# Layer one's key pieces split and stored by batch 0, and a new order of both mixers

## The chip, the cores and the metric

One core of one Trainium2 chip runs the kernel. The metric is the device time of one execution in microseconds; of the kernel before three runs are shown. The core's engines are TensorE (PE in the rows; its weight loads are PEld), VectorE (DVE), ScalarE (ACT), GpSimd (POOL) and SyncE (SP), which here issues all large DMAs, in order.

## What is computed

Two layers of a streaming encoder, on 1024 prompt frames and 8 streams of 16 frames, so 9 tiles of 128 tokens, of width 1024. Everything is float32.

```python
def trunk_layer(x, pos, cache_k, cache_v, pool_prev, conv_prev, ...):
    xn = rms_norm(x, norm_mix)
    q, k, v, u = mixer_inputs(xn, pos, w_in, q_gain, k_gain)   # 512 | 128 | 128 | 512 columns
    attn = window_attention_prompt(q, k, v, sinks)             # or sink_attention over the cache
    pool, new_pool = pool_mixer(u, pool_prev, w_pool, pool_scale)
    x = x + jnp.concatenate([attn, pool], axis=-1) @ w_out
    f, new_conv = conv_ffn(rms_norm(x, norm_ffn), conv_prev, w_up, conv_w, conv_b, w_down)
    x = x + f
```

`pool_mixer` takes running means over 2, 4, 8 and 16 frames; `conv_ffn` multiplies by w_up (1024 x 5632), convolves over 3 frames, gates and multiplies by w_down (2816 x 1024).

## The kernel before, in words

Every large product is made as three: each operand is split into a rounded high part and the remainder (`hi`, `lo`), and `mm3` (products at L154 to L156) issues hi x hi, hi x lo and lo x hi into one accumulator. A weight piece (128 x 512, or two 128 x 256 side by side) is loaded raw by SyncE (`w_dma`, L167; the load is at L218 or L227), cast to its high part by ScalarE (L184) or VectorE (L182) and subtracted by VectorE (L185): `w_split`. A piece with a key is then stored, both parts, 512 KB, in a scratch in DRAM (L188); the next time a piece of that key is wanted, it is loaded from there in one go (L179) and not split. `w_advance` keeps raw loads five pieces and splits three pieces ahead; there are 6 buffers of split pieces (`W`) and 5 raw ones.

Each layer is a mixer and then a feed-forward part of 21 up and 34 down units. The mixer takes the tiles in three batches of three. For batch b the units are called k{b} (query, key and value columns, 12 pieces: 8 of 512 columns and 4 pairs of 256), u{b} (pooling columns, 8 pieces), p{b} (pooling), L (steps of attention for all batches), o{b} (out projection, 16 pieces); n1 to n3 are the input norms of the batches with their transposes (norm multiply L258 on VectorE; the transposes at L278 are evacuated at L281 by ScalarE and L282 by VectorE), m0 to m2 the norms before the feed-forward part. s0 and s1 prepare the operands of its first products: sums and splits of 128 x 1152 (L314 on ScalarE, L315 and L323 on VectorE), and v and w are those products (their evacuations: L938). `par` loads the small parameters: gains (L1261, L1262), sinks (L1263, and L1265 eight times), the pool's scale (L1267), with small multiplies at L1268 to L1270. `sc` loads state rows (L1304), `cw` the convolution's weights (L1285, L1286).

The first three key pieces of batch 0 are used for tile 0, then tile 1, then tile 2, as their norms come (L362 on); from the fourth piece on a unit holds all three tiles.

What sets the order: every unit is a token with a number from `PLAN` (L65 to L68; a pair gives the first number and the step of a stream, `L` the numbers of the tiles, the `e_` entries choose VectorE, 1, or ScalarE, 0, for some copies; `e_w` says how many of every four weight pieces have their high part cast by VectorE, L1444). `arrange` (L45) takes the token with the least number whose forerunners (`pre`) are done. After that the framework's scheduler may shift instructions within each engine's order; each engine runs its own in order. The keys are given by `keyed` in the mixer's function. In layer one (l == 0) batch 0's key pieces get none, so batch 0 splits them and stores nothing, batch 1 loads and splits them again and stores them, and batch 2 loads the stored ones. In layer two, and for the u and o pieces of both layers, the first batch stores.

Of the kernel before, what the change touches and what calls it, by code (L numbers as in the profile page):

```python
# [44 lines left out]
def arrange(tokens, limits):  # L45
# [26 lines left out]
def encoder_kernel(ctx: ExitStack, tc: tile.TileContext, consts, x_prompt, x_sample, cache_k, cache_v,  # L72
# [1280 lines left out]
    for l in range(DEPTH):  # L1353
# [11 lines left out]

        def keyed(x, units, b, l=l):
            if l == 0 and x == "k" and b == 0:
                return units
            for i, w in enumerate(w for u in units for w in u.ws):
                w.key = l, x, i  # L1370
            return units
# [39 lines left out]
        n = [0] * 9  # L1411
# [104 lines left out]
```

## Time and profile before

| | us |
|---|---|
| three runs, median (lowest to highest) | 2229.7 (2226.32 to 2231.16) |
| the profiled execution, its own time | 2223.63 |
| its span in the profile | 2221.8 |
| TensorE busy in the span | 2157.7 (97%) |
| VectorE busy | 1705.8 (77%) |
| ScalarE busy | 966.2 (43%) |
| GpSimd busy | 326.8 (15%) |
| TensorE's clock, mean over the span | 0.995 of full |

Layer one's mixer takes about the first 400 us, layer two's lies between about 1000 and 1500; the rest is the feed-forward parts. Read the busy shares first, then the stretches in which TensorE is not busy, then what it waited for in each of them. A busy TensorE at a granted clock of 0.5 gets half as much done, so the clock's column belongs to the reading.

### The profile page before, as it was taken

What the parts mean: (1) busy time and instruction counts of PE and PEld (TensorE: products, weight loads), DVE (VectorE), ACT (ScalarE), POOL (GpSimd) and SP (SyncE); (2) the same over time, 40 slices, a digit from 0 to 9 for tenths busy, and PEclk for the clock granted to TensorE, in tenths of its full rate; (3) what the DMA queues carried; (4) which work ended last, traced back from release to release, by engine and by line L of the source; (5) the groups of instructions that cost most, each with busy time, mean ns of one, the idle gap of its engine ahead of it and who ended that gap; (6) DMA issues with size and microseconds to landing.
All of it is one profiled execution on the core that took longest, in us unless ns stands there. A gap on an engine that the chain in (4) does not pass through costs nothing.

```text
span 2221.8 us, 36068 instructions
## 1 busy us (share of the span) xinstructions
PE 2157.7 (97%) x13178; PEld 1935.6 (87%) x13178; DVE 1705.8 (77%) x3210; ACT 966.2 (43%) x1797; POOL 326.8 (15%) x499
## 2 busy tenths in 40 slices
PE   7999999999999999999999999989999999999999
PEld 6777867999999998878888887779999999988887
DVE  5775468998999998766556754699898999987663
ACT  4554356443434344443345544564343434353431
POOL 0100001112122323000000000012212232320000
PEclk9999999999999999999999999999999999999999
DMA  7667753222233437958675676532222343488563
GB/s 253 231 215 261 267 183 135 77 87 95 80 118 124 143 126 257 286 173 270 209 253 182 231 244 211 210 112 88 98 77 96 108 150 119 152 280 270 184 192 110
DMA packets 320036, 386.49 MB, mean 174 GB/s; under 512 B 21938, under 2 KB 224386, under 8 KB 319858
## 3 DMA queue, kind: packets, MB, share of 16 engines
q1 hardware_dynamic: 319858, 384.18, 52.3%
q8 instruction: 104, 1.70, 0.3%
q14 instruction: 74, 0.61, 0.1%
HBM read 274.73 MB, written 109.37 MB: 173 GB/s over the span
## 4 chain that ended last, share of the span: by engine, by line
PE 84%; DMA 6%; DVE 4%; ACT 2%; issue 2%; SPq 0%; POOL 0%; DVEq 0%; ACTq 0%; POOLq 0%
PE mm L154 15%; PE mm L156 15%; PE mm L155 15%; PE s L154 11%; PE s L156 11%; PE s L155 11%; PE s L653 2%; DMA B<-gd 1%; DMA raw<-in_w_down_dram 1%; PE tr L640 1%; DMA W<-wd0o 1%; PE tr L278 1%; PE mm L457 1%; PE s L601 1%; PE s L602 1%
## 5 line engine op out<-in xcount | busy, mean ns | idle before, releaser
L154 PE MATMUL mm<-B,W 128*128 128x288 f32 (+1 forms) x1376 | 419.7, 305 | 12.6 <-ACT B L314 10.7
L155 PE MATMUL mm<-B,W 128*128 128x288 f32 (+1 forms) x1376 | 417.8, 304 | 3.7 <-DVE B L315 3.7
L156 PE MATMUL mm<-B,W 128*128 128x288 f32 (+1 forms) x1376 | 417.1, 303 | 0.0
L154 PE MATMUL s<-B,B 128*128 128x512 f32 x704 | 279.1, 397 | 3.8 <-DVE u L1172 1.8
L156 PE MATMUL s<-B,B 128*128 128x512 f32 x704 | 278.6, 396 | 3.9 <-DVE B L1145 3.9
L155 PE MATMUL s<-B,B 128*128 128x512 f32 x704 | 277.9, 395 | 0.0
L154 PEld LDWEIGHTS mm<-B,W 128*128 128x128 f32 x1376 | 260.8, 190 | 17.0 <-ACT B L314 12.6
L155 PEld LDWEIGHTS mm<-B,W 128*128 128x128 f32 x1376 | 260.7, 189 | 5.9 <-DVE B L315 4.6
L156 PEld LDWEIGHTS mm<-B,W 128*128 128x128 f32 x1376 | 260.7, 190 | 0.7 <-issue 0.2
L986 DVE SCALAR_TENSOR_TENSOR B<-B,cvp,B 128x1168 f32<-128x1168 f32 x176 | 250.4, 1427 | 3.1 <-ACT B L984 2.8
L154 PE MATMUL mm<-W,B 128*128 128x512 f32 (+1 forms) x576 | 216.4, 383 | 11.8 <-ACT W L184 3.8
L156 PE MATMUL mm<-W,B 128*128 128x512 f32 (+1 forms) x576 | 215.2, 375 | 0.0
L155 PE MATMUL mm<-W,B 128*128 128x512 f32 (+1 forms) x576 | 214.2, 372 | 0.0
L879 ACT CAST W<-Q 128x512 fp32r<-128x512 f32 x132 | 82.1, 622 | 250.1 <-PE mm L156 166.0
L1144 ACT CAST B<-B 128x256 fp32r<-128x256 f32 (+1 forms) x128 | 97.2, 780 | 208.1 <-DMA B<-gd 70.0
L154 PE MATMUL s<-B,W 128*128 128x288 f32 x576 | 171.0, 297 | 0.0
L155 PE MATMUL s<-B,W 128*128 128x288 f32 x576 | 170.0, 295 | 0.0
L156 PE MATMUL s<-B,W 128*128 128x288 f32 x576 | 170.0, 295 | 0.0
L156 PEld LDWEIGHTS s<-B,B 128*128 128x128 f32 x704 | 132.5, 188 | 36.8 <-DVE B L1145 5.6
L154 PEld LDWEIGHTS s<-B,B 128*128 128x128 f32 x704 | 132.6, 188 | 36.5 <-ACT B L1144 5.2
L155 PEld LDWEIGHTS s<-B,B 128*128 128x128 f32 x704 | 132.6, 188 | 30.8
L880 DVE TENSOR_TENSOR W<-Q,W 128x512 fp32r<-128x512 f32 x132 | 135.8, 1030 | 17.3 <-ACT W L879 17.2
(234 smaller groups left out, 4856.9 us busy)
## 6 DMA issues: line engine op xcount, KB each, us to landing
raw<-in_w_up_dram SPq DMA_DIRECT2D x176, 256.0 KB
raw<-in_w_down_dram SPq DMA_DIRECT2D x154, 256.0 KB
gd<-B SPq DMA_DIRECT2D x44, 576.0 KB
B<-gd SPq DMA_DIRECT2D x32, 576.0 KB
W<-wd0o SPq DMA_DIRECT2D x32, 512.0 KB
W<-wd1o SPq DMA_DIRECT2D x32, 512.0 KB
raw<-in_w_in_dram SPq DMA_DIRECT2D x52, 256.0 KB
W<-wd1k SPq DMA_DIRECT2D x24, 512.0 KB
```

The costliest lines, as they stand in the source:

```text
L154: pe.matmul(out=out, lhsT=a[0], rhs=b[0], start=first, stop=False)
L155: pe.matmul(out=out, lhsT=a[0], rhs=b[1], start=False, stop=False)
L156: pe.matmul(out=out, lhsT=a[1], rhs=b[0], start=False, stop=last)
L278: pe.transpose(out=tr[:, (k - a) * 128:(k - a + 1) * 128], in_=xn[:, k * 128:(k + 1) * 128], identity=ident)
L457: pe.matmul(out=o, lhsT=w.raw, rhs=d, start=True, stop=True)
L601: pe.matmul(out=p[:, i, kr], lhsT=q[:, h], rhs=K[:, g, kr], start=True, stop=False)
L602: pe.matmul(out=p[:, i, kr], lhsT=q[:, h], rhs=K[:, 2 + g, kr], start=False, stop=True)
L653: pe.matmul(out=o, lhsT=V, rhs=H.pop(("p", g, kk)), start=kk == kks[0], stop=kk == 1)
L879: act.copy(out=hi, in_=src)
L880: dve.tensor_tensor(out=lo, in0=src, in1=f32(hi), op=ALU.subtract)
L986: dve.scalar_tensor_tensor(out=c, in0=h[:, j:j + 1168], scalar=cvp[:, j, ct:ct + 1], in1=c, op0=ALU.mult, op1=ALU.add)
L1144: act.copy(out=h, in_=f32(o))
```

## The change

It gives batch 0's key pieces of layer one their key as well: batch 0 splits and stores them, batches 1 and 2 load them. It sets the numbers of nearly all streams of both mixers anew, chooses the engine of some copies differently (in both layers key columns to VectorE, value columns to ScalarE; in layer one u columns to ScalarE, and every fourth cast of a weight piece to VectorE; in layer two `e_x1` to ScalarE and `e_x2` to VectorE), and makes the unit w.5 wait for `cw` and `sc`. Of the table the row of layer one is shown, and not that of layer two.

```diff
-    dict(k0=(12.35, 0.15), u0=(27.6, 1.13), k1=(35.46, 2.26), u1=(78.0, 4.62), o0=(92.76, 2.89), k2=(160.39, 1.54), u2=(167.47, 3.15), o1=(177.0, 4.09), o2=(235.74, 4.2), p0=(40.1, 3.5), p1=(86.68, 12.45), p2=(194.05, 11.9), n1=(-86.25, 2.26), n2=(26.8, 3.63), n3=(92.6, 1.1), m0=(218.99, 3.57), m1=(260.89, 0.13), m2=(181.58, 0.95), d=(-13.48, 3.86), L=(26.9, 49.72, 64.52, 85.45, 108.8, 144.29, 158.38, 183.7, 209.44, 245.41), cw=(259.88, 23.53), sc=(227.68, 60.94), s0=(257.44, 3.18), s1=(268.93, 2.61), v=(209.05, 0.65), w=(316.25, 1.16), upw=(342.36, 0.16), e_q=0, e_k=0, e_v=1, e_u=1, e_k2=1, e_qt=0, e_pt0=0, e_pt1=0, e_ps0=1, e_ps1=1, e_ks=0, e_w=0, e_x0=1, e_x1=0, e_x2=0),
+    dict(k0=(0.4, 2.37), u0=(34.1, 0.93), k1=(35.52, 2.03), u1=(80.99, 4.42), o0=(76.31, 4.58), k2=(160.39, 1.54), u2=(167.28, 3.02), o1=(177.22, 4.01), o2=(234.36, 9.42), p0=(40.1, 2.0), p1=(77.15, 12.45), p2=(193.68, 11.66), n1=(-114.15, 0.88), n2=(25.73, 3.64), n3=(96.31, 1.04), m0=(215.0, 3.57), m1=(265.16, 0.34), m2=(195.73, 0.23), d=(5.52, 6.56), L=(26.9, 49.72, 64.52, 85.8, 108.91, 144.29, 149.46, 186.79, 209.44, 245.41), cw=(351.65, 368.58), sc=(220.46, 49.37), s0=(257.44, 3.51), s1=(242.24, 0.26), v=(182.04, 25.01), w=(370.59, 1.67), upw=(408.93, 0.1), e_q=0, e_k=1, e_v=0, e_u=0, e_k2=1, e_qt=0, e_pt0=0, e_pt1=0, e_ps0=1, e_ps1=1, e_ks=0, e_w=1, e_x0=1, e_x1=0, e_x2=0),
...
@@ -1363,9 +1363,7 @@
                 q = list((pre or {}).get(i, ())) + ([f"{st}.{i - 1}"] if i else [])
                 add(f"{st}.{i}", k + i * step, u, q, (res or {}).get(i))
 
-        def keyed(x, units, b, l=l):
-            if l == 0 and x == "k" and b == 0:
-                return units
+        def keyed(x, units, l=l):
             for i, w in enumerate(w for u in units for w in u.ws):
                 w.key = l, x, i
             return units
@@ -1400,8 +1398,8 @@
             nn = f"n{b + 1}.5"
             kres = {7: {"qkv": 3}, 11: {"V": 3}}
             kpre = {0: [nn, f"k{b - 1}.11"], 11: ["par"]} if b else {0: ["n1.1"], 1: ["n1.3"], 2: ["n1.5"], 11: ["par"]}
-            stream(f"k{b}", keyed("k", kvq_units(l, b), b), kpre, kres)
-            stream(f"u{b}", keyed("u", u_units(l, b), b), {0: [nn] + (["d.9"] if l else []), 3: [f"p{b - 1}.3"] if b else [], 7: [f"p{b}.0"] + (["spl"] if b == 2 else [])}, {7: {"T6": -6}})
+            stream(f"k{b}", keyed("k", kvq_units(l, b)), kpre, kres)
+            stream(f"u{b}", keyed("u", u_units(l, b)), {0: [nn] + (["d.9"] if l else []), 3: [f"p{b - 1}.3"] if b else [], 7: [f"p{b}.0"] + (["spl"] if b == 2 else [])}, {7: {"T6": -6}})
             if b == 2:
                 toks[-5].pre += ("spl",)
             stream(f"p{b}", [pool_unit(l, b, g) for g in range(4)], {0: [f"u{b}.3", "par"], 2: [f"u{b}.7"]}, {0: {"T6": 3}})
@@ -1419,7 +1417,7 @@
             add(f"L.{i}", key, f, ([f"L.{i - 1}"] if i else ["par"] + (["d.9"] if l else [])) + list(pre), res)
             lastidx[t] = i
         for b in range(3):
-            ou = keyed("o", out_units(l, b), b)
+            ou = keyed("o", out_units(l, b))
             pre = {0: [f"p{b}.3"], 4: [f"L.{lastidx[3 * b + 2]}"]}
             stream(f"o{b}", ou, pre, {15: {"T6": -6}})
         for nm, f1, f2, pre in (("cw", conv_load, conv_cols, []), ("sc", sconv_load, sconv_cols, [kc1])):
@@ -1434,7 +1432,7 @@
             add(f"upw{i}", pl["upw"][0] + pl["upw"][1] * i, lambda l=l, i=i: up_advance(l, i), ["o2.10"])
         for s, k in ((0, "v"), (1, "w")):
             for n, x in enumerate((0, 1, 7, 4, 8, 10, 2)):
-                pre = [f"s{s}.{x}", "o2.15"] + ([f"{k}.{n - 1}"] if n else ["v.6"] if s else [])
+                pre = [f"s{s}.{x}", "o2.15"] + ([f"{k}.{n - 1}"] if n else ["v.6"] if s else []) + (["cw", "sc"] if s and n == 5 else [])
                 add(f"{k}.{n}", pl[k][0] + pl[k][1] * n, up_first(l, s, n), pre)
         ev = arrange(toks, {"T6": 18, "qkv": 4, "V": BUFS["V"]})
         for t in ev:
```

In counts, over the whole program: raw loads of key pieces 52 before, 40 now; loads of split layer-one key pieces 12 before, 24 now, stores of them 12 in both; subtractions at L185 84 before, 72 now; casts at L182 (VectorE) 8 before, 19 now, at L184 (ScalarE) 76 before, 53 now; copies of u columns on VectorE 8 before, none now. TensorE's products are the same in number.

SyncE at the beginning, before (`raw` are weight pieces in the order of use, `snk`, `gain` and `V` the parameters, `B` the input):

```order
9 L1349 DMA cst<-in_consts_dram 128x464
10 L1261 DMA gain<-in_q_norm_dram 128x64
11 L1262 DMA gain<-in_k_norm_dram 128x64
12 L1263 DMA snk<-in_attn_sinks_dram 128x8
13 L1265 DMA snk<-in_attn_sinks_dram 16x1 x8
14 L1267 DMA V_268<-in_pool_scale_dram 4x128
15 L218 DMA raw_276<-in_w_in_dram 128x512
16 L247 DMA B_250<-in_x_prompt_dram 128x1024
17 L247 DMA B_252<-in_x_prompt_dram 128x1024
18 L247 DMA B_254<-in_x_prompt_dram 128x1024
19 L218 DMA raw_278<-in_w_in_dram 128x512
```

The same place now:

```order
9 L1349 DMA cst<-in_consts_dram 128x464
10 L218 DMA raw_250<-in_w_in_dram 128x512
11 L218 DMA raw_252<-in_w_in_dram 128x512
12 L1261 DMA gain<-in_q_norm_dram 128x64
13 L1262 DMA gain<-in_k_norm_dram 128x64
14 L1263 DMA snk<-in_attn_sinks_dram 128x8
15 L1265 DMA snk<-in_attn_sinks_dram 16x1 x2
16 L188 DMA wd0k_86<-W_254 128x1024
17 L218 DMA raw_258<-in_w_in_dram 128x512
18 L1265 DMA snk<-in_attn_sinks_dram 16x1
19 L188 DMA wd0k_87<-W_260 128x1024
20 L218 DMA raw_264<-in_w_in_dram 128x512
```

The fourth and fifth raw pieces have moved ahead of the parameters, and from then on a store of a split key piece (`wd0k`) stands ahead of each further raw load.

VectorE ahead of batch 1's norms, before, from the evacuation of the first u columns on (raw_633, raw_689 and raw_691 are batch 1's first key pieces; `sA` and `D` belong to pooling):

```order
60 L149 COPY u_645<-mm_544 128x384
61 L185 TENSOR_TENSOR W_733<-raw_633,W_733 128x512
62 L282 TENSOR_TENSOR B_614<-tr_622,B_611 128x3x128
63 L414 COPY uh<-u_645 128x15
64 L425 TENSOR_TENSOR sA_659<-u_645 128x398
65 L149 COPY u_655<-mm_551 128x384
66 L185 TENSOR_TENSOR W_763<-raw_689,W_763 128x512
67 L429 SCALAR_TENSOR_TENSOR D_662<-sA_659,u_645 128x384
68 L414 COPY uh<-u_655 128x15
69 L185 TENSOR_TENSOR W_858<-raw_691,W_858 128x512
```

The same place now, from the split of the first u piece that stands behind the rotary step of tile 0 (raw_476 and raw_506 are u pieces):

```order
64 L185 TENSOR_TENSOR W_693<-raw_476,W_693 128x512
65 L414 COPY uh<-u_754 128x15
66 L425 TENSOR_TENSOR sA_768<-u_754 128x398
67 L414 COPY uh<-u_764 128x15
68 L429 SCALAR_TENSOR_TENSOR D_771<-sA_768,u_754 128x384
69 L185 TENSOR_TENSOR W_744<-raw_506,W_744 128x512
70 L436 TENSOR_TENSOR D_771<-sA_768,cst 128x15
71 L437 TENSOR_TENSOR D_771<-D_771,u_754 128x15
72 L425 TENSOR_TENSOR sA_846<-u_764 128x398
73 L400 MEMSET u_873 128x15
74 L149 CAST B_590<-tr_591 128x4x128
```

The splits of key pieces and the copies of u columns are gone from between the pooling steps. Before, 26 of the subtractions at L185 stand ahead of the second tile's first evacuation in batch 1 and 30 ahead of the third tile's last; now it is 20 and 20. Of the copies of u columns 4 stood there, of casts at L182 none; now it is none and 6.

VectorE at the end of layer one's mixer, before (the first three rows are the last norms' multiplies, L938 evacuates first products, L315 and L323 are the second half's sums and splits):

```order
620 L258 SCALAR_TENSOR_TENSOR B_3915<-B_3556,st_3916,B_3309 128x1024
621 L258 SCALAR_TENSOR_TENSOR B_3921<-B_3558,st_3922,B_3309 128x1024
622 L258 SCALAR_TENSOR_TENSOR B_3927<-B_3560,st_3928,B_3309 128x1024
623 L938 TENSOR_TENSOR B_4029<-mm_4016,PT_4011 128x288
624 L938 TENSOR_TENSOR PT_4011<-s_4034,PT_4011 128x288
625 L938 TENSOR_TENSOR PT_4065<-mm_4052,PT_4011 128x288
626 L938 TENSOR_TENSOR PT_4011<-mm_4071,PT_4011 128x288
627 L938 TENSOR_TENSOR B_4085<-mm_4071,PT_4065 128x288
628 L938 TENSOR_TENSOR B_4085<-s_4087,PT_4065 128x288
629 L938 TENSOR_TENSOR B_4029<-mm_4101,PT_4011 128x288
630 L315 TENSOR_TENSOR B_4116<-B_3725,B_4115 128x1152
631 L315 TENSOR_TENSOR B_4120<-B_3733,B_4119 128x1152
```

The same place now:

```order
613 L258 SCALAR_TENSOR_TENSOR B_3919<-B_3538,st_3920,B_3234 128x1024
614 L258 SCALAR_TENSOR_TENSOR B_3925<-B_3540,st_3926,B_3234 128x1024
615 L938 TENSOR_TENSOR B_3987<-mm_3974,PT_3911 128x288
616 L938 TENSOR_TENSOR PT_3911<-s_3992,PT_3911 128x288
617 L315 TENSOR_TENSOR B_4007<-B_3653,B_4006 128x1152
618 L938 TENSOR_TENSOR PT_4055<-mm_4042,PT_3911 128x288
619 L315 TENSOR_TENSOR B_4011<-B_3661,B_4010 128x1152
620 L938 TENSOR_TENSOR PT_3911<-mm_4061,PT_3911 128x288
621 L938 TENSOR_TENSOR B_3987<-mm_4091,PT_3911 128x288
622 L315 TENSOR_TENSOR B_4015<-B_3945,B_4014 128x1152
623 L880 TENSOR_TENSOR W_4172<-raw_4149,W_4172 128x512
624 L938 TENSOR_TENSOR B_3987<-mm_4119,PT_3911 128x288
```

The first two splits of the second half stand between the evacuations and no longer behind all of them; two evacuations of the first half (`mm_4061` again, and `s_4077`) have gone behind the sums.

## Rows read from the trace of the kernel before

**Rows 1.** The page's first part: busy us of each engine, share, instructions.
```profile
PE 2157.7 (97%) x13178; PEld 1935.6 (87%) x13178; DVE 1705.8 (77%) x3210; ACT 966.2 (43%) x1797; POOL 326.8 (15%) x499
```

**Rows 2.** Stretches of 25 us; columns: us, busy (instructions) by engine, PEclk, DMA share, GB/s.
```profile
0.00:25.00 25.00, 12.50 (x48) 9.81 (x49) 11.93 (x25) 11.15 (x21) 1.97 (x8) 0.93 0.73 256
...
50.00:75.00 25.00, 22.92 (x135) 20.64 (x133) 23.02 (x72) 14.31 (x35) 2.91 (x2) 1.00 0.77 270
...
375.00:400.00 25.00, 18.23 (x104) 15.98 (x103) 23.86 (x29) 14.34 (x22) 2.69 (x5) 0.86 0.04 11
...
1450.00:1475.00 25.00, 22.27 (x140) 19.32 (x139) 24.21 (x31) 13.62 (x28) 6.03 (x6) 1.00 0.47 157
1475.00:1500.00 25.00, 19.01 (x124) 17.35 (x123) 23.64 (x29) 14.39 (x20) 0.00 (x0) 0.86 0.06 17
```

**Rows 3.** Timeline of SyncE at the beginning: start, us, engine, line, operation, count.
```profile
9.31 4.90 SPq L1265 DMA_DIRECT2D snk<-in_attn_sinks_dram  x8
...
14.66 0.36 SPq L218 DMA_DIRECT2D raw<-in_w_in_dram  x1
```

**Rows 4.** Timelines of ScalarE, VectorE, TensorE, 16 to 19 us; in brackets idle before, releaser.
```profile
17.48 0.62 ACT L184 CAST W<-raw 128x512 fp32r<-128x512 f32 x1 [2.30 <-DMA raw<-in_w_in_dram]
...
16.50 1.28 DVE L258 SCALAR_TENSOR_TENSOR B<-B,st,B 128x1024 f32<-128x1024 f32 x1 [0.67 <-POOL st L257]
...
18.15 0.79 PE L154 MATMUL mm<-W,B 128*128 128x512 f32 x1 [3.00 <-ACT W L184]
18.75 1.48 PE L278 MATMUL tr<-cst,B 128*128 128x128 f32 x6
```

**Rows 5.** Stretches of 2 us at the beginning; columns as in group 2.
```profile
18.00:20.00 2.00, 1.85 (x8) 1.67 (x8) 1.87 (x2) 0.48 (x2) 0.47 (x1) 0.50 1.02 381
```

**Rows 6.** Stretches holding batch 1's first key pieces, layer one, then layer two.
```profile
64.00:88.00 24.00, 19.57 (x95) 14.99 (x94) 21.58 (x77) 13.69 (x41) 4.52 (x3) 0.93 0.27 94
1171.00:1191.00 20.00, 19.01 (x102) 14.68 (x101) 14.88 (x47) 10.98 (x25) 0.55 (x1) 1.00 0.18 59
```

**Rows 7.** Timeline of TensorE in batch 1's stage of layer one.
```profile
75.70 0.60 PE L278 MATMUL tr<-cst,B 128*128 128x128 f32 x2 [2.15 <-DVE B L282]
```

**Rows 8.** Groups of one line: count, lowest/median/highest ns, first and last start.
```profile
L184 ACT CAST W<-raw x76: 602/621/642, 8.0 to 1274.0; 128x512 fp32r<-128x512 f32 x76
...
L185 DVE TENSOR_TENSOR W<-raw,W x84: 658/691/694, 8.7 to 1275.3; 128x512 fp32r<-128x512 f32 x84
...
L182 DVE CAST W<-raw x8: 418/427/428, 1023.0 to 1264.2; 128x512 fp32r<-128x512 f32 x8
...
L149 DVE COPY u<-mm x8: 541/554/558, 53.2 to 166.8; 128x384 f32<-128x384 f32 x8
...
L188 SPq DMA_DIRECT2D wd0k<-W x12: 326/472/1301, 54.8 to 99.3; - x12
```

**Rows 9.** The DMA view, 0 to 66 us: totals, and two kinds of issues.
```profile
DMA packets 9638, 17.71 MB, mean 268 GB/s; under 512 B 1507, under 2 KB 5290, under 8 KB 9633
...
raw<-in_w_in_dram SPq DMA_DIRECT2D x28, 256.0 KB
...
wd0k<-W SPq DMA_DIRECT2D x5, 512.0 KB
```

**Rows 10.** A stretch of layer two's batch 0; columns as in group 2.
```profile
1136.00:1148.00 12.00, 12.00 (x63) 10.47 (x62) 10.06 (x22) 5.79 (x12) 2.18 (x2) 1.00 1.05 395
```

**Rows 11.** Timelines of SyncE, VectorE and TensorE at the ends of both mixers.
```profile
324.73 7.68 SPq L1304 DMA_DIRECT2D B<-in_state_conv_dram  x8
...
329.78 0.17 DVE L1269 TENSOR_SCALAR snk<-snk 128x8 f32<-128x8 f32 x1 [4.96 <-DMA snk<-in_attn_sinks_dram]
...
381.02 0.40 PE L154 MATMUL mm<-B,W 128*128 128x288 f32 x1 [1.73 <-ACT B L314]
...
1446.53 0.15 DVE L256 TENSOR_SCALAR st<-st 128x1 f32<-128x1 f32 x1 [2.02 <-ACT B L255]
...
1487.17 0.61 PE L154 MATMUL mm<-B,W 128*128 128x288 f32 x1 [3.93 <-ACT B L314]
```

More of the change, by code (lines that the diff above doesn't have):

```diff
@@ L67 @@
-    dict(k0=(-43.86, 0.15), u0=(49.49, 0.1), k1=(26.26, 4.1), u1=(76.32, 4.61), o0=(81.16, 2.69), k2=(139.16, 1.11), u2=(150.18, 5.15), o1=(175.45, 5.19), o2=(244.07, 2.25), p0=(49.92, 3.56), p1=(56.81, 4.29), p2=(193.02, 12.48), n1=(-18.93, 0.85), n2=(30.53, 4.46), n3=(92.15, 1.8), m0=(222.0, 1.72), m1=(234.28, 0.33), m2=(278.02, 1.14), d=(-24.93, 3.08), L=(26.9, 49.72, 64.52, 87.91, 106.15, 148.52, 158.51, 180.13, 216.19, 239.71), cw=(264.41, 12.12), sc=(273.99, 6.32), s0=(264.1, 2.08), s1=(276.75, 4.45), v=(278.27, 0.1), w=(272.47, 516.37), upw=(298.18, 0.41), e_q=0, e_k=0, e_v=1, e_u=0, e_k2=0, e_qt=0, e_pt0=0, e_pt1=0, e_ps0=1, e_ps1=1, e_ks=0, e_w=1, e_x0=0, e_x1=1, e_x2=0),
+    dict(k0=(0.4, 2.37), u0=(34.1, 0.93), k1=(35.52, 2.03), u1=(80.99, 4.42), o0=(76.31, 4.58), k2=(160.39, 1.54), u2=(167.28, 3.02), o1=(177.22, 4.01), o2=(234.36, 9.42), p0=(40.1, 2.0), p1=(77.15, 12.45), p2=(193.68, 11.66), n1=(-114.15, 0.88), n2=(25.73, 3.64), n3=(96.31, 1.04), m0=(215.0, 3.57), m1=(265.16, 0.34), m2=(195.73, 0.23), d=(5.52, 6.56), L=(26.9, 49.72, 64.52, 85.8, 108.91, 144.29, 149.46, 186.79, 209.44, 245.41), cw=(351.65, 368.58), sc=(220.46, 49.37), s0=(257.44, 3.51), s1=(242.24, 0.26), v=(182.04, 25.01), w=(370.59, 1.67), upw=(408.93, 0.1), e_q=0, e_k=1, e_v=0, e_u=0, e_k2=1, e_qt=0, e_pt0=0, e_pt1=0, e_ps0=1, e_ps1=1, e_ks=0, e_w=1, e_x0=1, e_x1=0, e_x2=0),
@@ new lines @@
+    dict(k0=(-19.1, 0.17), u0=(41.72, 0.11), k1=(23.93, 4.64), u1=(76.32, 4.66), o0=(81.16, 2.69), k2=(131.41, 2.01), u2=(159.64, 3.19), o1=(176.74, 5.16), o2=(244.45, 2.2), p0=(50.37, 3.79), p1=(41.63, 2.14), p2=(196.59, 14.02), n1=(-19.61, 0.67), n2=(28.93, 4.45), n3=(97.64, 0.29), m0=(224.51, 0.88), m1=(254.53, 0.73), m2=(277.92, 1.14), d=(-24.93, 2.65), L=(26.9, 49.72, 64.52, 88.15, 105.43, 151.29, 160.24, 182.14, 217.23, 240.57), cw=(253.91, 4.74), sc=(274.24, 6.92), s0=(251.59, 2.11), s1=(265.4, 3.05), v=(280.44, 0.1), w=(269.22, 13783.52), upw=(276.35, 0.22), e_q=0, e_k=1, e_v=0, e_u=0, e_k2=0, e_qt=0, e_pt0=0, e_pt1=0, e_ps0=1, e_ps1=1, e_ks=0, e_w=1, e_x0=0, e_x1=0, e_x2=1),
```

## The prediction

> **What bounds the kernel now.** I began with the busy shares: TensorE is busy 2157.7 of a span of 2221.8 us [rows 1], so 64 us are to be had on it at most, by removing its waits. The table of 25-us stretches says where they lie. The long stages of both feed-forward parts read 25.00 of 25; what is missing lies in the first 25 us (12.50 busy, clock 0.93), at 50 to 75 (22.92), and where a mixer ends: 375 to 400 (18.23, clock 0.86) and 1450 to 1500 (22.27, then 19.01 at clock 0.86) [rows 2]. From 50, 375 and 1450 us on VectorE is nearly full, 23.02, 23.86 and 24.21 of 25: there it sets the pace, and a microsecond taken from it ahead of a late operand is worth about one. ScalarE (14 us of 25) is bound nowhere.
>
> Then the timelines. At the beginning SyncE issues eight tiny loads of sinks from 9.31 to 14.21 and only at 14.66 the next weight load [rows 3]. That piece lands at 17.48, where ScalarE had waited 2.30 us for it, and TensorE stands 3.00 us, until 18.15 [rows 4]; from 18 to 20 its clock is then granted at 0.50, which is 1.2 GHz, the lower of the two levels, where it takes double time [rows 5]. In batch 1's query-key-value stage TensorE is busy 19.57 of 24 us at a clock of 0.93, with VectorE at 21.58 of 24; the same stage of layer two, whose weights had been split and stored by batch 0, reads 19.01 of 20 at 1.00, VectorE 14.88 of 20 [rows 6]. The longest gap there, 2.15 us before 75.70, waits for VectorE's evacuation of transposes (L282) [rows 7]. So this stage is held by VectorE, not by weights or by TensorE.
>
> **The change, part by part.** *Splits.* Batch 1's 12 key pieces are no longer split. Off VectorE go 12 subtractions of 691 ns (8.3 us), off both engines 12 casts, and the new numbers shift casts and evacuations: on VectorE 11 more casts of 427 ns (+4.7) and 8 fewer u evacuations of 554 ns (-4.4), on ScalarE 23 fewer casts of 621 ns (-14.3) [rows 8]. VectorE's sum is -8.0 us. ScalarE's part I cost at nothing: it is covered by TensorE, and ScalarE is not full.
>
> What counts is what stands ahead of batch 1's norms on VectorE. By the order, ahead of the first evacuation of the second tile's transposes stand 6 subtractions fewer (-4.1), 4 u evacuations fewer (-2.2) and 6 casts more (+2.6): -3.8 us. Ahead of the last of the third tile's it is 10 subtractions fewer: -6.9 - 2.2 + 2.6 = -6.5 us, and some pooling and attention operations moved behind them. Both are more than the 2.15 us gap. The worth is bounded by the stage itself: idle 24 - 19.57 = 4.4 us, and 0.07 of 24 us lost to the clock, 1.7: together 6.1. Layer two's stage keeps 0.99 idle in 20, that is 1.2 in 24, at full clock. I take the difference, **-5.0**, since batch 1 then runs as it does there; ends 0 and -6.1. If VectorE is no longer late, the next in line is ScalarE's evacuation of the same transposes, then the loads below.
>
> *Loads and stores.* Twelve stores of 512 KB move from batch 1 (54.8 to 99.3 us [rows 8]) into batch 0, and batch 1 loads 12 x 512 KB in place of 12 x 256 KB: 3.1 MB more in all. That is little; when it is moved matters. Up to 66 us, the start of batch 1's first key piece, the queue has moved 17.71 MB (a mean of 268 GB/s), with 5 of those stores and 28 raw pieces among it [rows 9]. Now 12 stores (+7 x 0.524 = +3.67), 5 loads of split weights (+2.62) and 24 raw pieces (-4 x 0.262 = -1.05) come before it: 22.95 MB, which in 62 us is 370 GB/s. In layer two's batch 0 the same mix ran at 395 GB/s with TensorE busy 12.00 of 12 [rows 10]. So it fits with 6% to spare, and a load can find itself behind a store of 512 KB (1.3 us at 395). I take **+1.0**; ends 0 and +14.5 (at 285 GB/s, near the 268 of the stretch before: 22.95 / 285 = 80.5 us against 66).
>
> The Trainium skill (DMA: Bandwidth & Descriptors, Bandwidth) says that a transfer between HBM and SBUF is bound by about 358 GB/s for a core. By it, the 22.95 MB need an estimated 64 us, and batch 1 would start no earlier than now. The trace disagrees with it as a ceiling: 395 GB/s stood for 12 us [rows 10].
>
> *Beginning.* The fourth and fifth raw pieces are issued ahead of the parameters, at about 5.4 us instead of 14.66; the landing took 2.8 us (14.66 to 17.48), so the 3.00 us wait for it goes. Late next is the second tile's norm (L258), which ended at 16.50 + 1.28 = 17.8 [rows 4]. On VectorE it now stands behind a cast, a subtraction and the multiply on the sinks (L1269), whose load is issued two weight loads later (0.8 us); but no longer behind the one on the pool's scale (L1270). I put its end at 16.2 to 17.8. TensorE, which took that tile's transposes at 18.75, then takes them 1 to 2.5 us earlier. If the gap becomes short enough, the clock's fall (about 1.7 us in 3.4) goes too. I take **-2.0**; ends 0 and -3.7. The 12 stores now wait on SyncE ahead of the raw loads behind them; a store and the next raw load wait for the same split, so this costs nothing while five pieces are ahead; without that cover, it is in the +14.5 above.
>
> *End of layer one's mixer.* VectorE stood 4.96 us at 324.8 for a load of sinks (L1269) with two operations of attention and norm behind it [rows 11]; in the new order these stand ahead of it. The first two splits of the second half's sums (L315) move ahead of three evacuations, so TensorE's waits for such splits (1.73 us before 381.02 for L314 [rows 11]) shrink. Against it, the load of the tenth out-weight goes behind eight state loads that take SyncE 7.68 us from 324.73 [rows 11], and two evacuations of the first half now stand behind all eleven sums. Gain at most 5 (half of the 6.8 us idle and 3.5 us of clock in [rows 2]), loss at most 7.7 (the whole of SyncE's 7.68). I take **-2.0**, near the gain, as the loads are one and the sums many.
>
> *End of layer two's mixer.* VectorE idles 2.02 us before 1446.53 for a norm with the sums behind it, and TensorE waits 3.93 us before 1487.17 for a split [rows 11]. The first three sums now come before that norm. **-1.5**; ends 0.5 more and -4. The rest of the new numbers leaves TensorE's order as it was, from batch 2 to the end of the mixer and in the long stages: nothing.
>
> **Sum.** -5.0 + 1.0 - 2.0 - 2.0 - 1.5 = -9.5 us against the profiled execution: its own time is 2223.63 us (span 2221.8 and 1.8 around it), so 2214.1. The median of the three runs is 2229.7, 6.1 above that execution; I carry the difference over: **2220.2**, say 2220.0. A measurement of this kernel tells about 0.2%, 4.5 us, from no change.
>
> **Rivals.** *A, transfers become the bound of batch 0 (slower).* TensorE would stand for weights from about 25 us on. What decides is the rate: batch 1 starts at 22.95 MB over it, and the other terms give back 5.0 + 3.5 = 8.5 us, so it is slower than before when the start comes later than 74.5 us, below 308 GB/s. At 285 it is +14.5 - 8.5 = +6.0: 2235.7. For it: the mean before was 268, and stores and raw loads stand on one queue. Against it: 395 in layer two, and the mean of before was not for want of rate.
>
> *B, transfers hold batch 0 at about 350 GB/s.* Start of batch 1 at 65.6, as before; the -2.0 is lost and little else: 2229.7 - 8.5 + 1 = 2222. That is what the page's rule would give within a microsecond.
>
> *C, VectorE stays late at batch 1.* The pooling chain and the casts that the new numbers put on VectorE fill the place; the 5.0 falls to 1: 2224.
>
> *D, the end of layer one goes wrong.* The tenth out-weight comes 7.7 us late, with the sums behind it: -9.5 + 2 + 7.7 = +0.2: 2230, no change.
>
> **How the numbers follow.** The forecast has 0.47, B 0.13, C 0.15, D 0.13, A 0.12. The forecast's own range is 2209 (terms near their better ends, -5.5 - 3 - 4 - 3 = -15.5, less 5 for the spread of the runs) to 2224; B and C lie within it. To hold 8 in 10 it reaches up to 2231, past D, and leaves out A's upper part and a tenth below. Faster by over 0.2% (under 2225.2): nearly all of the forecast, B and most of C: 0.73. Within: D and what is left: 0.15. Slower: A: 0.12.
>
> **What would show it.** Right: the wait before the fourth piece's first matmul gone and the tile-1 transposes before 18; the stage of batch 1 beginning by 64 and reading under 1.5 us idle in 24 at clock 1.00; DMA at 350 to 390 GB/s from 12 to 64 us; VectorE under 20 of 25 in 50 to 75. Wrong: TensorE waiting for raw or split-weight loads between 25 and 90 us (A, B); the L282 gap still there (C); a wait of several us for an out-weight near 330 (D).

## The result, and the profile after

The changed kernel takes a median of 2214.62 us (2212.91 to 2218.74, six runs) against 2230.22 (2225.57 to 2231.16, six runs) for the one before, run beside it: a ratio of 0.9941, with an interval of 0.9931 to 0.9951. By the ratio that is 13.2 us less (11 to 15.4); the medians lie 15.6 apart. It is 5.4 below the predicted 2220.0, inside the range. The two profiled executions took 2223.63 and 2214.03 us: 9.6 less, where the sum had said 9.5. Yet the sum came out by terms that missed on both sides, and its largest term came about in another way than it was argued.

The page of the changed kernel, first part (span; busy us, share and instructions of each engine), to be held against [rows 1]:

```profile
span 2212.3 us, 36010 instructions
...
PE 2153.8 (97%) x13178; PEld 1933.4 (87%) x13178; DVE 1695.2 (77%) x3201; ACT 956.3 (43%) x1782; POOL 325.3 (15%) x499
```

TensorE's busy time fell by 3.9 us and its idle time by 5.6 (span less busy, 64.1 before, 58.5 now): waits are the larger part of the gain.

Stretches of the changed kernel (columns as in [rows 2]), which answer to [rows 2, 5, 6]:

```profile
0.00:25.00 25.00, 11.23 (x41) 8.53 (x42) 11.88 (x25) 9.25 (x17) 2.46 (x8) 0.93 0.80 301
25.00:50.00 25.00, 25.00 (x156) 22.61 (x155) 13.67 (x28) 10.73 (x24) 2.52 (x2) 1.00 1.01 367
50.00:75.00 25.00, 25.00 (x147) 23.05 (x146) 22.04 (x78) 14.96 (x44) 3.90 (x3) 1.00 0.82 293
...
375.00:400.00 25.00, 19.08 (x128) 18.25 (x127) 24.48 (x34) 12.89 (x18) 2.04 (x6) 0.86 0.15 43
1450.00:1475.00 25.00, 20.59 (x150) 18.15 (x148) 23.19 (x33) 17.45 (x33) 3.02 (x6) 1.00 0.34 105
1475.00:1500.00 25.00, 21.63 (x140) 21.07 (x141) 24.06 (x32) 12.39 (x17) 2.08 (x6) 0.86 0.16 47
64.00:88.00 24.00, 23.51 (x119) 18.80 (x118) 19.88 (x67) 13.20 (x39) 3.24 (x2) 1.00 0.58 199
20.00:22.00 2.00, 2.00 (x6) 1.61 (x5) 1.96 (x3) 0.50 (x2) 0.01 (x1) 0.51 1.04 415
125.00:150.00 25.00, 23.29 (x116) 17.13 (x114) 21.02 (x79) 16.75 (x52) 4.01 (x2) 1.00 0.45 146
```

Batch 1's stage, 64 to 88, now reads 23.51 of 24 at a clock of 1.00 (19.57 at 0.93 in [rows 6]). From 25 to 75 TensorE has no idle time, though the queue carries 367 GB/s for the first half of it. The first 25 us are no better than before, and the clock still falls, now at 20 to 22.

The same points on TensorE's line, found by counting products, show where the gain arises. The last two columns are profiles of two kernels from the experiments below: the kernel before once more, and the change with layer two's old numbers, whose layer one is that of the change.

| us from the span's start | before | after | lead | before, once more | layer one alone |
|---|---|---|---|---|---|
| batch 0, end of its 48th product | 31.02 | 31.43 | -0.4 | 32.18 | 29.67 |
| batch 1, first product of its first key piece | 66.11 | 68.10 | -2.0 | 67.27 | 66.34 |
| end of that piece's last product, with the third tile | 88.21 | 81.33 | 6.9 | 88.84 | 79.56 |
| batch 2, first key product | 194.24 | 188.02 | 6.2 | 195.15 | 186.24 |
| end of layer one's mixer | 403.23 | 393.92 | 9.3 | 402.72 | 395.98 |
| layer two, first key product of batch 1 | 1171.90 | 1161.94 | 10.0 | 1171.64 | 1162.47 |
| end of layer two's mixer | 1499.93 | 1490.35 | 9.6 | 1499.33 | 1491.90 |

(Batch 1's first key product comes 2.0 us later; 1.6 of them are other work of the new order that stands ahead of it.) From the first of these points to batch 2 the change gains 6.6 us in the first pair of profiles and 6.4 in the second, so that part is firm. Of the beginning and of the stretch from batch 2 to the end of layer one's mixer this can't be said: there two profiles with the same layer one differ by 1.8 us (31.43 and 29.67) and by 3.8 us (205.90 and 209.74).

The DMA view of the changed kernel, 0 to 66 us (totals and two kinds of issues), for [rows 9]:

```profile
DMA packets 10367, 21.80 MB, mean 330 GB/s; under 512 B 1587, under 2 KB 5431, under 8 KB 10362
...
wd0k<-W SPq DMA_DIRECT2D x12, 512.0 KB
raw<-in_w_in_dram SPq DMA_DIRECT2D x20, 256.0 KB
```

And the groups of one line, for [rows 8]; their counts are those of the order:

```profile
L184 ACT CAST W<-raw x53: 603/621/646, 10.3 to 1264.0; 128x512 fp32r<-128x512 f32 x53
...
L185 DVE TENSOR_TENSOR W<-raw,W x72: 660/688/695, 9.9 to 1265.3; 128x512 fp32r<-128x512 f32 x72
...
L182 DVE CAST W<-raw x19: 416/420/428, 8.4 to 1254.0; 128x512 fp32r<-128x512 f32 x19
...
L188 SPq DMA_DIRECT2D wd0k<-W x12: 326/348/1403, 12.9 to 41.2; - x12
```

The timelines of TensorE, VectorE and SyncE at the beginning, for [rows 3, 4]:

```profile
10.06 1.54 PE L278 MATMUL tr<-cst,B 128*128 128x128 f32 x6 [10.06 <-DVE B L258]
...
16.23 0.50 PE L154 MATMUL mm<-W,B 128*128 128x512 f32 x1 [1.35 <-ACT W L184]
19.08 0.85 PE L278 MATMUL tr<-cst,B 128*128 128x128 f32 x6 [2.35 <-DVE st L256]
...
8.39 0.43 DVE L182 CAST W<-raw 128x512 fp32r<-128x512 f32 x1 [2.76 <-DMA raw<-in_w_in_dram]
...
16.98 0.17 DVE L1269 TENSOR_SCALAR snk<-snk 128x8 f32<-128x8 f32 x1 [1.71 <-DMA snk<-in_attn_sinks_dram]
17.06 0.68 DVE L185 TENSOR_TENSOR W<-raw,W 128x512 fp32r<-128x512 f32 x1
17.66 1.28 DVE L258 SCALAR_TENSOR_TENSOR B<-B,st,B 128x1024 f32<-128x1024 f32 x1
...
5.86 2.13 SPq L218 DMA_DIRECT2D raw<-in_w_in_dram  x2
...
10.33 0.33 SPq L1263 DMA_DIRECT2D snk<-in_attn_sinks_dram  x1
```

The fourth piece is in time now (a wait of 1.35 for its split in place of 3.00). But the second tile's norm ends at 18.94 (at 18.27 in layer one alone), where [rows 4] had 17.78 and four more profiles of kernels that begin as the one before 18.2 to 18.8: VectorE waits 1.71 us for the sinks, then splits a piece, then multiplies.

TensorE at the ends of both mixers, for [rows 11]:

```profile
327.24 0.51 PE L154 MATMUL mm<-W,B 128*128 128x512 f32 x1 [0.50 <-DMA W<-wd0o]
...
379.76 0.61 PE L154 MATMUL mm<-B,W 128*128 128x288 f32 x1 [3.64 <-ACT B L314]
...
1475.95 0.40 PE L154 MATMUL mm<-B,W 128*128 128x288 f32 x1 [3.65 <-ACT B L314]
```

The tenth out-weight costs half a microsecond; the wait for a split in layer two is 3.65 where it was 3.93.

### The profile page after: what moved, and what is told of

It reads as the page before. It is cut to its first block, busy times and chain, and to the rows that moved or that the text cites. A ratio compares the mean times of both kernels' runs of the same rounds, so it can differ in the third digit from the quotient of the medians.

```text
span 2212.3 us, 36010 instructions
## 1 busy us (share of the span) xinstructions
PE 2153.8 (97%) x13178; PEld 1933.4 (87%) x13178; DVE 1695.2 (77%) x3201; ACT 956.3 (43%) x1782; POOL 325.3 (15%) x499
## 4 chain that ended last, share of the span: by engine, by line
PE 84%; DMA 7%; DVE 6%; ACT 2%; issue 1%; SPq 1%; DVEq 0%; POOL 0%; ACTq 0%
PE mm L154 15%; PE mm L155 15%; PE mm L156 15%; PE s L154 11%; PE s L156 11%; PE s L155 11%; PE s L653 2%; DMA raw<-in_w_down_dram 1%; PE tr L640 1%; DMA B<-gd 1%; DMA W<-wd0o 1%; DMA snk<-in_attn_sinks_dram 1%; PE tr L278 1%; PE s L601 1%; PE mm L457 1%
```

## The experiments

By the first pair of profiles batch 1's stage was freed and nothing else of size happened. Open was by what: by the key pieces' splits leaving VectorE, as predicted (theory 1), by the new numbers (theory 2), or by the engine choices (theory 3). In the expectations, which were written ahead of each run, theory A is theory 1, B and E are theory 2, and D is theory 3; the prediction's rivals A to D are other things.

**Parts of the change by themselves.** Before, with the keys alone:

```diff
-            if l == 0 and x == "k" and b == 0:
-                return units
```

> The numbers of before, with batch 0's key pieces of layer one stored (and loaded by batch 1). Theory A (the gain is VectorE's: no splits ahead of batch 1's norms): the stage of batch 1's first key pieces loses its 2.15 us gap before the second tile's transposes and its slow clock, 5 to 8 us less than before, about 2223 where before is 2230; queue rate up to 66 us near 350 GB/s. Theory B (the gain is the new order of both mixers): within 2 us of before, and the gap stays. Rival C (stores beside raw loads hold batch 0 when the order was not set for them): slower than before by 2 us or more, with TensorE waiting for raw pieces between 20 and 45 us.

And the reverse, the changed kernel with batch 0's key pieces of layer one left without their key, so that batch 1 splits and stores its own:

```diff
-            stream(f"k{b}", keyed("k", kvq_units(l, b)), kpre, kres)
+            stream(f"k{b}", kvq_units(l, b) if l == 0 and b == 0 else keyed("k", kvq_units(l, b)), kpre, kres)
```

> The changed kernel with batch 0's key pieces of layer one unkeyed again: batch 1 loads them raw, splits and stores them, with the new numbers. Theory A: 6 to 9 us above the changed kernel, about 2222, the gaps of batch 1's stage back, VectorE over 22.5 of 25 us there. Theory B: within 2 us of the changed kernel (2215).

Keys alone: ratio 0.9984 (0.9974 to 0.9994), 2224.97 us. Numbers and engine choices without the keys: 0.9949 (0.9935 to 0.9964), 2217.97. So of 13.2 us some 11.4 (8.0 to 14.5) come without a single split leaving batch 1. The keys' own 3.6 (1.3 to 5.8) lie between what theory 1 (5 to 8) and theory 2 (under 2) had expected. TensorE's timeline and the stretches of the keys-only kernel show that the stage stays held:

```profile
72.99 0.84 PE L278 MATMUL tr<-cst,B 128*128 128x128 f32 x6 [2.38 <-DVE st L618]
```

```profile
25.00:50.00 25.00, 25.00 (x153) 22.17 (x153) 13.60 (x26) 13.03 (x29) 2.52 (x2) 1.00 1.05 407
...
64.00:88.00 24.00, 21.21 (x101) 16.02 (x101) 22.41 (x79) 13.93 (x41) 3.69 (x3) 0.93 0.37 144
```

VectorE is at 22.41 of 24 without the splits: what stood behind them moved up. Ahead of the second norm's multiply stand 6 subtractions and 5 pooling steps fewer than before, but 13 other operations more, 11 of them of attention; it begins at 71.57, where it began at 70.31. The stretch of the kernel without the keys is free, with all splits in it and VectorE fuller than in the changed kernel:

```profile
64.00:88.00 24.00, 23.76 (x120) 19.15 (x120) 22.90 (x73) 14.19 (x40) 3.58 (x2) 1.00 0.48 161
```

Theory 1 falls as the main cause. How full VectorE is does not decide; what stands ahead of the norms does.

**Layer by layer.** The changed kernel with layer two's old row of numbers, and before with layer two's new row (the second row of the table, exchanged whole):

```diff
 PLAN = [
...
-    dict(k0=(-19.1, 0.17), ...
+    dict(k0=(-43.86, 0.15), ...
```

> The whole change except layer two's numbers, which are those of before. By the profiles (layer two's mixer ends 9.6 us earlier where it began 10.0 earlier) both theories expect the same time as the changed kernel within 1.5 us, 2214 to 2216. If layer two's numbers bring the 1.5 us that the prediction gave them, 2216 to 2217.

> The kernel before with layer two's numbers alone. By the profiles within 1.5 us of before, 2229 to 2231; by the prediction's term for the end of layer two's mixer 1.5 us less. A rival for the part of the measured gain that the profiles don't show (13 us by the ratio, 9.6 by the two profiles): layer two's order makes executions steadier, then 3 us or more under before.

Layer one alone: 0.9959 (0.9943 to 0.9975), 2220.00; layer two's numbers alone: 0.9978 (0.9967 to 0.9989), 2225.08. By timed runs layer two's row is worth 4.9 us (2.5 to 7.4), and 4.0 by the distance of layer one alone from the change. Its profiled execution took 2223.01, 0.6 less than that of before. In pairs of profiles that differ in this row alone, the time from batch 1's first key product to the end of layer two's mixer is 327.69 and 327.03 (on the kernel before), 329.44 and 328.41 (on the change): 0.7 and 1.0 us. The traces show no place for the rest.

**Engine choices.** The changed kernel with layer one's old choices, and before with the new ones:

```diff
-e_k=1, e_v=0, e_u=0, ... e_w=1
+e_k=0, e_v=1, e_u=1, ... e_w=0
```

> The changed kernel with layer one's choice of engines as before (key and value columns, u columns on VectorE, no casts of weight pieces on VectorE). Theory D (the stage of batch 1 is freed because the u evacuations leave VectorE): 4 us or more above the changed kernel, and the gap for the second tile's transposes is back. Theory E (it is freed by the places that the new numbers give to the norms and the pooling steps on VectorE): within 2 us of the changed kernel, 2213 to 2217; the first transposes begin 1.4 us earlier as the cast ahead of the first norm is gone.

> The kernel before with layer one's new choice of engines and nothing else. Theory D: 4 to 6 us less than before, 2223 to 2225. Theory E: within 2 us of before, 2227 to 2231.

Old choices in the changed kernel: 0.9939 (0.9926 to 0.9951), 2214.10, the same as the change. New choices alone: 1.0012 (1.0003 to 1.0021), and the gap stands:

```profile
76.41 0.44 PE L278 MATMUL tr<-cst,B 128*128 128x128 f32 x2 [2.14 <-DVE B L282]
```

Theory 3 falls. That leaves the numbers, of which two narrower sets were tried on the kernel before.

**Which numbers.** First the six streams ahead of batch 1, then one stream, the norms of batch 1, alone:

```diff
-k0=(12.35, 0.15), u0=(27.6, 1.13), k1=(35.46, 2.26), p0=(40.1, 3.5), n1=(-86.25, 2.26), n2=(26.8, 3.63)
+k0=(0.4, 2.37), u0=(34.1, 0.93), k1=(35.52, 2.03), p0=(40.1, 2.0), n1=(-114.15, 0.88), n2=(25.73, 3.64)
```

> The kernel before with the new numbers of six streams of layer one (k0, u0, k1, p0, n1, n2), nothing else; splits and engines as before. Theory E: batch 1's first key stage ends 5 us or more earlier than in the profile of before (88.2), and the time is 4 to 7 us less, 2222 to 2225. Theory A (splits) or D (engines): less than 2 us.

```diff
-n2=(26.8, 3.63)
+n2=(25.73, 3.64)
```

> The kernel before with one pair of numbers changed in layer one: n2 from (26.8, 3.63) to (25.73, 3.64), as in the change; splits, stores, engines and every other number as before. In VectorE's order the multiply of batch 1's second norm (L258) moves from row 110 to row 79, ahead of 12 pooling steps, still behind 24 of the 26 subtractions. Theory E (the place of the norm): batch 1's first key stage ends by 83 instead of 88, its 2.15 us gap is gone, and the time is 3 to 6 us less than before, 2223 to 2226. Theory A (the splits) or a need for all six streams together: less than 2 us, and the gap stays.

Six streams: 0.9978 (0.9969 to 0.9987), 2223.42. One stream: 0.9999 (0.9988 to 1.0010), 2227.51. Both free the stage: the last product of batch 1's first key piece ends at 79.27 and 81.00, against 88.21 before and 81.33 in the change. In the one-number kernel VectorE's multiply for the second norm of batch 1 has 79 instructions ahead of it in place of 110; among them are 8 pooling steps in place of 20, and still 24 of 26 subtractions. Of the other instructions that went behind it 13 are of attention, 2 are copies of u columns and 2 fill u's first columns. It begins at 61.46 and not at 70.31. Which of these counted most was not separated. But the gain does not last. Stretches of the one-number kernel, and its TensorE timeline:

```profile
64.00:88.00 24.00, 23.65 (x121) 18.95 (x121) 23.19 (x83) 15.64 (x45) 3.31 (x2) 1.00 0.51 165
...
125.00:150.00 25.00, 20.47 (x90) 14.02 (x89) 15.20 (x53) 13.42 (x36) 1.96 (x1) 0.86 0.50 179
```

```profile
135.86 1.23 PE L640 MATMUL tr<-cst,B 128*128 128x128 f32 x8 [2.68 <-DVE B L630]
138.69 0.69 PE L565 MATMUL tr<-cst,ks 128*128 128x128 f32 x2 [1.60 <-ACT PT L151]
```

Attention of batch 1 is now late at 135 us: two waits and a lower clock. Before, the stretch read:

```profile
125.00:150.00 25.00, 23.45 (x116) 17.46 (x115) 15.60 (x57) 12.93 (x36) 1.96 (x1) 1.00 0.59 207
```

The gain is used up: batch 2 begins at 194.46, where it began at 194.24 before. With six streams it is the same, in part (the same stretch):

```profile
125.00:150.00 25.00, 20.85 (x95) 14.84 (x93) 16.59 (x65) 14.42 (x43) 3.04 (x2) 0.86 0.52 194
```

8.9 us won at the stage, 2.8 left at batch 2 (191.46); 1.6 of both were won at the beginning already, by the 48th product. In the change this stretch reads 23.29 at 1.00: there the first products of the out-projection (o0, whose number went from 92.76 to 76.31) begin at 102.8 and no longer at 124.8, and u1 stands behind them, so TensorE has work between the attention's steps. That this is what keeps the gain is argued and not shown: o0's number was not tried by itself, and other numbers behind the stage (u1, p1, n3) changed with it.

**The price of the stores.** The changed kernel with each of batch 0's 12 key pieces stored a second time, to scratch memory that nobody reads (6.3 MB more; it adds transfers and no computation):

```diff
+    wsx = {(0, "k", i): dp.tile([128, 2, 512], F32, name=f"wx{i}") for i in range(12)}
...
+            if w.key in wsx:
+                sync.dma_start(out=wsx[w.key], in_=f32(g))
```

> The changed kernel with each of batch 0's 12 split key pieces of layer one stored twice, the second time to a scratch that nobody reads: 6.3 MB more between 12 and 42 us, where the queue already runs at 367 GB/s. If the transfers of batch 0 are hidden with little to spare (the prediction's 6%): the rate stays under 425 GB/s, TensorE waits for raw pieces, batch 1's first key piece begins 6 to 12 us later than the 68.1 of the changed kernel, and the time is 4 to 10 us more, 2219 to 2225. If raw loads five pieces ahead and the slack of batch 0 cover it: under 2 us more.

1.0010 (0.9998 to 1.0021), 2230.61: 16 us more than the change, all of its gain. Its stretches:

```profile
25.00:50.00 25.00, 21.80 (x128) 19.15 (x128) 10.79 (x23) 9.35 (x21) 0.77 (x2) 0.93 0.99 372
50.00:75.00 25.00, 21.68 (x129) 19.32 (x127) 21.10 (x73) 14.41 (x43) 4.68 (x3) 1.00 0.98 367
```

The DMA engines are full, and TensorE waits for splits of raw pieces that land late: rival A, called up by hand. Batch 1 begins at 77.69, 9.6 us later than in the change. Behind it, 7.5 are left at batch 2; the other half of the 16 arises later, with waits for out-weights from 334 us on, and 5.1 us of it in layer two's mixer, where this program's instructions stand in another order between 1360 and 1420 us of the change's time. That half is not explained by the stores.

**The beginning.** The changed kernel with the sinks' first load ahead of the second load of constants and of the fourth piece, and the casts of the first six pieces all on ScalarE:

```diff
+            if l:
...
+        sync.dma_start(out=snk[:, 0], in_=attn_sinks[0].partition_broadcast(128))
...
-            w.dve = i % 4 < pl.get("e_w", 0)
+            w.dve = i % 4 < pl.get("e_w", 0) and not (l == 0 and i < 6)
```

> The changed kernel with the sinks' first load issued ahead of the second table load and the fourth raw piece, and the first six pieces' casts on ScalarE. If the beginning gained nothing because VectorE first casts a piece ahead of the first norm and then waits 1.71 us for the sinks ahead of the second: first transposes at 8.6 to 9.0 instead of 10.06, second tile's by 17.3 instead of 19.08, no fall of the clock, 2 to 3.5 us less, about 2211.5 to 2213. If another wait takes their place (ScalarE's second piece, the raw loads, the pool's step of the norm): less than 1 us.

0.9932 (0.9919 to 0.9944), 2213.61: the lowest median of all, but not to be told from the change. TensorE's timeline shows the second tile's transposes 1.4 us earlier, with no wait worth the name, and the clock is granted at 1.00 in 20 to 22, as it is in the profile of layer one alone, which begins as the change does:

```profile
17.65 0.85 PE L278 MATMUL tr<-cst,B 128*128 128x128 f32 x6 [0.19 <-DVE st L256]
...
303.47 0.58 PE L601 MATMUL s<-B,Q 128*128 128x256 f32 x1 [2.18 <-DVE st L605]
327.64 0.50 PE L154 MATMUL mm<-W,B 128*128 128x512 f32 x1 [1.85 <-DMA W<-wd0o]
```

Batch 1 begins 2.6 us earlier than in the change, and 0.8 earlier than in layer one alone. The two later waits are longer than in the change (0.63 and 0.50), but in layer one alone they are too (1.26 and 0.77). From batch 2 to the end of layer one's mixer the three profiles take 210.2 (early sinks), 205.9 (the change) and 209.7 us (layer one alone); so what the early sinks win at the beginning, and whether it is lost here, is not to be told from one profile.

**The rest of the waits at 303 and 327.** Early sinks, layer one's old engine choices, and the eight state loads behind the tenth out-weight:

```diff
-sc=(220.46, 49.37)
+sc=(236.0, 34.0)
```

> The changed kernel with three edits to layer one: the engines as before (by the earlier run no loss, and no cast ahead of the first norm), the sinks' first load early, and the eight state loads behind the tenth out-weight and the inputs. If each wait that it takes away is worth its length: the second tile's transposes at 17 to 17.7, no wait for an out-weight between 322 and 330 (0.8 to 2.1 us before), 2 to 4 us less than the changed kernel, 2211 to 2213. If the waits are taken over by the next one, as when the early sinks alone gave 1 us of 2.6: 2212.5 to 2214.5.

0.9956 (0.9940 to 0.9971), 2218.03: worse, where 2211 to 2214.5 had been expected. The out-weight's wait is gone, the one before 305.79 is still 2.15 (for L605 on VectorE). But layer one's mixer ends at 396.38, 0.7 us behind that with the early sinks; most of the loss arises in layer two's mixer, which takes 332.01 us from batch 1's first key product to its end, against 328.41 in the change. Its instructions stand in another order between 1360 and 1420 us of the change's time, the same as in the kernel with the stores twice, though none of its numbers were changed, and TensorE waits there:

```profile
1412.68 0.67 PE L154 MATMUL mm<-W,B 128*128 128x512 f32 x1 [2.60 <-DVE B L460]
```

So this run says little on the state loads.

**Before, once more**, unchanged, for a second profile:

> The kernel before, once more, for a second profile of it. Its profiled execution (2223.6) lies under nearly all of its timed runs (medians of 2229 to 2230), that of the changed kernel (2214.0) does not (2214.6). If that execution was a fortunate one: 2226 to 2232 here, and batch 1's key stage again ends near 88, while the surplus lies elsewhere; if the surplus lies in layer two's mixer, it explains why layer two's numbers alone measured 4.9 us less though the profiles showed 0.6.

2223.12 us, with the stage's end at 88.84. So both profiled executions of before (2223.63 and 2223.12) lie 5 to 7 us below the medians of its timed runs (2228.65 to 2230.22), while that of the change lies 0.6 below its own. Of the timed gain some 4 to 6 us are therefore not in the traces.

## Why the prediction was right, and where it was not

*Total.* The profiles differ by 9.6, the sum said 9.5. That they meet so closely is luck: terms of the sum missed by 1 to 2 us each way, and profiles of one layer one differ by as much. The further 4 to 6 us of the timed runs come from the step "I carry the difference over": before's 6.1 between profile and median was taken for a property of both kernels, and the change has 0.6. Why before's timed runs lie above its profiles stays open.

*Batch 1, -5.0: right in place and near in size (-6.9 at its end, -6.2 kept to batch 2), wrong in cause.* That the stage was held by VectorE ahead of the norms, and that freeing it would bring it to layer two's picture, held: 0.49 us idle in 24 at full clock. What failed is "what counts is what stands ahead of batch 1's norms", as it was then counted: in subtractions, casts and u evacuations (-3.8 and -6.5 us), with the pooling steps named in half a sentence. Taking six subtractions away left a wait of 2.38, as other steps took their places; moving 31 instructions behind the norm, 12 of them pooling steps, 13 of attention and only 2 subtractions, removed it. "Batch 1 then runs as it does there" also left out what comes after: the stage's gain is lost at 125 to 150 us where the rest of the order stays as it was. The order between the stage and batch 2, which had no term, decided whether 6 us or none were kept.

*Loads and stores, +1.0: nothing was paid.* TensorE was busy 25.00 of 25 in both stretches. 21.80 MB had moved by 66 us, against 22.95 in the sum: 20 raw pieces had been issued by then, where the sum had 24 (4 x 0.262 = 1.05 MB). That there was little to spare held: 6.3 MB more, which at 370 GB/s are 17 us, delayed batch 1's start by 9.6, so the stretch could cover some 7. The Trainium skill (DMA: Bandwidth & Descriptors, Bandwidth) puts the limit of a core at about 358 GB/s; the same section says that this is each core's share when both cores of a pair stream, and that a single core was measured at up to 425. One core ran here, and the traces agree with the second: the keys-only kernel moved 407 for 25 us, and layer two 395 for 12 [rows 10]. The kernel with twice the stores, bound by its transfers, ran at 372 and 367.

*Beginning, -2.0: nothing came in the change's profile, some of it in others.* The wait for the fourth piece shrank as said. The step that failed is "I put its end at 16.2 to 17.8": 18.94. The sinks' load was issued at 10.33 and not 8.03, 2.3 us later where the sum had 0.8, because the two pieces ahead of it hold SyncE for 2.13; and a split stands between the sinks and the norm. With layer one's old engine choices the same norm ran from 16.25 to 17.53. The end of batch 0's 48th product tells the beginnings apart: 31.02 to 32.41 in five profiles of kernels that begin as the one before; 31.43, 29.67 and 29.26 in three that begin as the change (itself, layer one alone, the stores twice); 28.81 with the old engine choices, 28.78 with the early sinks. By the means, 31.7 and 30.1, some 1.6 us came, no more than the spread; the last two, one profile each, have 2.9. So more was to be had, and layer one's new engine choices, by which a cast and a split stand on VectorE ahead of that norm, seem to have taken it. But the totals of the change and of the last two lie within 1.0 us (2214.62, 2214.10, 2213.61), each with an interval 4 to 6 us wide, so what it would be worth at the end is not known.

*End of layer one's mixer, -2.0: not shown.* In the first pair of profiles it is -2.4 from the 1134th product (at 357.68 before) to the mixer's end, 45.55 and 43.16 us. The second pair has 44.79 and 44.63. That the first meets the term is luck. What failed is "TensorE's waits for such splits shrink": on the second half's products those over 0.3 us sum to 6.3 us before and 6.0 now, with one of 3.64. Rival D did not come: 0.50 us at the out-weight.

*End of layer two's mixer, -1.5: -0.7 and -1.0* in the pairs that differ in layer two's numbers alone. "The first three sums now come before that norm" moved the work, but the wait for a split stayed (3.93 to 3.65). The timed 4.9 us of layer two's numbers are not accounted for.

*The long stages, at nothing: some 2 us came there.* From the 1501st product to the 5801st, which is layer one's feed-forward part and the start of layer two, seven profiles of kernels that store no key pieces in layer one's batch 0 take 673.2 to 674.7 us (before 674.5), seven of kernels that do 671.0 to 672.4 (the change 672.3, the keys alone 671.9). The largest of the waits that shrank, before and after:

```profile
952.48 0.48 PE L154 MATMUL s<-B,B 128*128 128x512 f32 x1 [1.84 <-DVE u L1172]
...
943.31 0.47 PE L154 MATMUL s<-B,B 128*128 128x512 f32 x1 [0.78 <-ACT B L1144]
```

Why the keys matter so far from their place stays open.

*Rivals.* C (VectorE stays late) is what the keys alone do: 2224.97 against its 2224. A and B were not met: no wait for a load of weights from 25 to 90 us. Of the signs named for being right the stage's idle time held (0.49 us at a clock of 1.00). The others did not, or in part: the wait for the fourth piece is 1.35, the second tile's transposes come at 19.08, the stage begins at 68.1, the queue ran at 340 GB/s from 12 to 64 us, and VectorE is at 22.04 of 25 in 50 to 75.

## What to carry to other kernels

Where an engine with a full queue holds up another, list everything in its queue ahead of the late operand, and price moving each behind it: here 31 instructions put behind the norm, most of them pooling and attention, counted, and 6 splits taken away did not, as others took their places, though the splits were the change's purpose. A stage that is freed hands its gain to the next place where the same chain is late, so look there in the same view, and ask what else the waiting engine could do at that place. Compare a profile with a second one of the same kernel before a difference of a few microseconds is read from it, between two stages as much as between profile and timed runs.

## What had not been expected of the hardware

The first load's landing differs between executions of the same beginning. The multiply for the first norm (L258), which waits for a load that SyncE issues at 1.65 us, began at 7.29, 7.48, 7.67, 8.04 and 8.50 in five profiles of kernels that begin as the one before does. The profile that the prediction went by was the earliest of the five, so 1.2 us of any comparison at the beginning is this spread.

Transfers near the limit are not all alike: with 12 stores of 512 KB among the loads the queue moved 407 GB/s for 25 us with TensorE fully busy (keys alone), with 24 of them (stores twice) 372 and TensorE standing 3.2 us of 25. Whether the stores themselves lower the rate was not separated from the order of the loads.
